# Second half of the recurrence's r and the mLSTM's q and k: blocks of 256 features, with the high and the low input side by side in one product of 512 columns

## The chip, the core and the metric

The kernel runs on one core of a Trainium2 chip. The metric is the device time of one execution in microseconds (us). TensorE (PE in the profile) does the matrix products, VectorE (DVE) and ScalarE (ACT) do the elementwise work, GpSimd (POOL) some small steps, and SyncE (SP) issues the loads of the weights.

## What is computed

One decoder layer in float32, for 256 tokens of 2048 features. This case touches its first part, where one big product `proj = h @ w_in` is cut into columns for two token mixers:

```python
h = rms_norm(x, mix_pre_norm)
proj = h @ w_in
mlstm_p, rwkv_p, gate_p = split_cols(proj, (MLSTM_TOTAL, RWKV_TOTAL, GATE_TOTAL))
q, k, v, o, ir, fr = split_cols(mlstm_p, MLSTM_COLS)          # q, k: 512 columns each
rp = rwkv_p + (shift_right(rwkv_p, 1) - rwkv_p) * mu
r, kr, vr, wl, al, gl = split_cols(rp, RWKV_COLS)             # r, kr, vr: 1024 columns each
...
hm = mlstm_chunkwise(q, k, v, ig, logf)
y = rwkv7_scan(r_h, heads(decay), kr, v_h, kk, kk * a_h)
```

Behind it come the merge of the mixers, cross-attention and a large feed-forward part.

## The kernel before

**Precise products from two halves.** Weights and inputs are split into a high and a low part (`wh`, `wl` and `hx`, which holds `hh` and `hl`; 128x1024 values of weights are one *source*, 512 KB). ACT casts `wh` out of the loaded `raw` (L437), DVE subtracts to get `wl` (L463). Three products are then summed in a PSUM bank: high weights with high input, high with low, low with high. In a feature-major block (`fm`) the weights are the stationary operand and the 256 tokens are the moving columns, so each of the three has 256 columns. In the narrow form a block is 512 features: 8 sources of two 128-row slices (k), and 24 products per source. Token-major blocks (`tm`) move the weights instead, 512 columns at a time.

**The wide form** is used later in the program, by the feed-forward blocks (`fx`) and by `w_mw`: `hx` has high and low input next to each other, so one product of 512 columns covers high weights with both, and one of 256 columns adds low weights with high input. A wide block is 256 features: 4 sources of four k slices, and 16 products per source. Its bank holds two partial sums (for each 128 features), so its evacuation is longer: ACT copies one half out of PSUM, DVE adds the other (function `whole`), and then multiplies.

**Order of the work.** The first blocks are: the small gates (`tm`, 296 columns), r (2 narrow blocks), kr (2), vr (2), q and k of the mLSTM (1 narrow block each, `q_evac`), then v and o (`tm`), the gates and the branches. Sources are numbered in this text from the first one of r: r has 0 to 15, kr 16 to 31, vr 32 to 47, q and k 48 to 63. `Feed` runs ahead: when a source is multiplied, the `wl` of the third one after it is queued on DVE.

**Banks.** The accumulators of these blocks come from a pool of four PSUM banks (`acc`). A narrow or a wide block takes two of them, so a block can only begin when the evacuation of the block two places before it has left its banks.

**Side work.** Everything else (evacuations, the preparation of the recurrence in `k_group`, one for each of four groups of 256 features, and `inverses`) is cut into pieces by generators, and the class `Spread` decides while the program is written out where a piece stands: at each `side.half` at most a few pieces, as long as its budgets for DVE and ACT are positive. It writes pieces out at once, however many there are, where one is needed: `work(b)` begins with `side.need(pend[-2])`, which writes out all that is left of the evacuation two blocks back, and `q_evac` itself starts with

```python
yield from side.patience(tasks["k"], 12)
```

which lets up to 12 pieces pass and then writes out what is left of the last `k_group`. In `k_group`, `kk`, `nr`, `k2` and `ep` are parts of the tile `kt`; a maximum over the head sums `ssk` (from PE) is followed by a logarithm and an exponential on ACT, then by products on DVE that fill `KR` and `BK`, and the scaling of `rr`. `inverses` begins with the products `gramA` of `KR` and `BK` on PE.

Each engine works through its own queue in the order that this made.

Of the kernel before, what the change touches and what calls it, by code (L numbers as in the profile page):

```python
# [15 lines left out]
P = 128  # L16
D = 2048
S = 256
# [136 lines left out]
def _layer(ctx, tc, nc, d, dbg):  # L155
# [9 lines left out]
    def U(name, shape=None, dt=F32):  # L165
        return mp.tile(shape or [P, 8, S], dt, tag="U", bufs=7, name=name)
# [98 lines left out]
    def times(out, ps, row):  # L265

        if len(ps.shape) == 3:
            row = bc(row, ps.shape[1])
        dve.tensor_mul(apart(out), halves(ps), apart(row))

    def whole(ps):

        us, lo = T2("us"), T2("ul")
        for i in range(2):
            act.copy(lo[:, i], ps[i][:, 1])
        for i in range(2):
            dve.tensor_add(us[:, i], ps[i][:, 0], lo[:, i])
        return us

    def bc(ap, n):  # L280
        return ap.unsqueeze(1).broadcast_to((ap.shape[0], n, ap.shape[1]))
# [100 lines left out]
    def block(kind, srcs, xs, evac, before=None, cols=512, pool_=None, pre=None, bankwise=False, tail=0,  # L382
              two=False, wide=None):


        blocks.append(dict(kind=kind, srcs=srcs, xs=xs, evac=evac, before=before, cols=cols,
                           pool=pool_ or acc, pre=pre, task=None, bankwise=bankwise, tail=tail, two=two, wide=wide is not None, xw=wide))
        return blocks[-1]
# [218 lines left out]
    def W(name, blk):  # L607
        return [d[name][blk, c] for c in range(d[name].shape[1])]
# [241 lines left out]

    def r_evac(hf):
        def gen(ps):
            if hf == 0:
                M["rr"] = U("rr")
            for g in range(2):
                pr = PR()
                times(pr, ps[g], st0.rb)
                yield
                for j in range(2):
                    p = hf * 4 + g * 2 + j  # L860
                    shiftmix(M["rr"][:, p], pr[:, j], p)
                yield
        return gen

    def k_evac(hf):
        def gen(ps):
            if hf == 0:
                M["KR"] = big("KR", [P, 8, 4, 2, 64])
                M["BK"] = big("BK", [P, 8, 4, 2, 64])
            kr = M["BK"].rearrange("p a c s t -> p a (c s t)")  # L870
            for g in range(2):
                pr = PR()
                times(pr, ps[g], st0.rb)
                yield
                for j in range(2):
# [304 lines left out]
            tasks["hb"] = side.add(hb_split(), back=True)  # L1180


    def q_evac(i):
        def gen(ps):
            if i == 0:
                yield from side.patience(tasks["k"], 12)
                M["qk"] = U("qk")
            qk = M["qk"]
            for g in range(2):
                o = qk[:, i * 4 + g * 2:i * 4 + g * 2 + 2]  # L1190
                times(o, ps[g], st0.rb)
                yield
            if i == 1:
                side.need(tasks["gates"])
                for _ in range(3):
                    yield
                for h in range(4):
                    q = aux("sc", [P, 384])
                    for jt in range(2):
                        mm(q[:, jt * 256:jt * 256 + 256 - jt * 128], qk[:, 4 + h, jt * 128:(jt + 1) * 128],  # L1200
                           qk[:, h, jt * 128:256])
                    dve.scalar_tensor_tensor(M["pw"][:, h], q, 128 ** -0.5, M["pw"][:, h], op0=ALU.mult, op1=ALU.mult)
                    yield
        return gen
# [294 lines left out]


    block("tm", [d["op"][c, :, :, S:] for c in range(8)], xs0, sm_evac, cols=NSM, pre=pre_sm)
    for hf in range(2):
        block("fm", W("w_in", hf), xs0, r_evac(hf), pre=pre_r0 if hf == 0 else None)
    for hf in range(2):
        block("fm", W("w_in", 2 + hf), xs0, k_evac(hf))
    for hf in range(2):
        block("fm", W("w_in", 4 + hf), xs0, v_evac(hf))

    def drain_bulk():
        while side.bulk:  # L1510
            side._piece(side.bulk[0])

    block("fm", W("w_in", 6), xs0, q_evac(0))
    block("fm", W("w_in", 7), xs0, q_evac(1), )
    for n in range(2):
        block("tm", W("w_in", 8 + n), xs0, vm_evac(n))
    for n in range(2):
        o1 = block("tm", W("w_in", 10 + n), xs0, o_evac(n))

    def need_hb():  # L1520
        for hf in range(2):
# [31 lines left out]
    for i in range(2):  # L1553
        for cb in range(4 + AHEAD):
            if cb >= AHEAD:
                before = None
                if cb == AHEAD:
                    before = need_hb if i else lambda: side.need(o1["task"])
                br = gated(i, cb - AHEAD, before)
            if cb < 4:  # L1560
                block("tm", W("w_in", 12 + i * 4 + cb), xs0, gate_evac(i, cb))
    br["before"] = start_mem

    def load_x():
# [365 lines left out]
def _pairs(w):  # L1930

    return w.reshape(w.shape[0], -1, 256, 2).transpose(0, 1, 3, 2).reshape(w.shape)
# [17 lines left out]
def prepare(i):  # L1950
    f = {k: np.asarray(v) for k, v in i.items()}
    w = f["w_in"][0]
    o = {}
    feat = lambda v: np.ascontiguousarray(v.reshape(S, KD, P).transpose(2, 1, 0))
    o["x"], o["mem"] = feat(f["x"]), feat(f["mem"])
    o["x"] = np.ascontiguousarray(o["x"].reshape(P, 8, 2, S).transpose(1, 0, 2, 3))
    par = np.zeros((P, NPAR), np.float32)

    def put(n, v, rows=P):
        par[:rows, PC[n]:PC[n] + v.shape[1]] = v  # L1960

# [24 lines left out]
    smw = smw.reshape(D, NSM // 2, 2).transpose(0, 2, 1).reshape(D, NSM)  # L1986
    smw = smw.reshape(8, 2, P, NSM).transpose(0, 2, 1, 3)
    o["op"] = np.concatenate([o.pop("x"), smw], 3)
    o["w_s0"] = np.concatenate([par[:, PC["mixg"]:PC["mixg"] + 16], smw[0, :, 0]], 1)
    ga, gb = w[:, 6440:8488], w[:, 8488:10536]  # L1990
    o["w_in"] = _blocks(np.concatenate([w[:, 3080:6152], w[:, 0:1024], _pairs(np.concatenate([w[:, 1024:3072], ga, gb], 1))], 1), 512)
    o["w_up"] = f["rwkv_w_up"][0]
    o["a_up"] = f["rwkv_a_up"][0]
    o["g_up"] = f["rwkv_g_up"][0]
    o["w_br"] = np.concatenate([_blocks(_pairs(f[n][0]), 512) for n in ("w_branch_a", "w_branch_b")], 0)
    o["w_mo"], o["w_mw"] = _blocks(f["w_mix_out"][0][:, :512], 512), _blocks(f["w_mix_out"][0][:, 512:], 256)
    kv = f["xattn_wkv"][0]
    o["w_xk"], o["w_xv"] = _blocks(kv[:, :512], 512), _blocks(_pairs(kv[:, 512:]), 512)
    o["w_xq"] = _blocks(f["xattn_wq"][0], 512)
    o["w_xo"] = _blocks(f["xattn_wo"][0], 512)  # L2000
    fu = f["ffn_w_up"][0].reshape(D, 2, DFF)
    cut = lambda a, b, n: fu[:, :, a:b].reshape(D, 2, -1, n).transpose(0, 2, 1, 3).reshape(D, -1)
    o["w_fu"], o["w_fw"] = _blocks(cut(0, 768, 256), 512), _blocks(cut(768, DFF, P), 256)
    o["w_fd"] = _blocks(_pairs(f["ffn_w_down"][0]), 1024)
    return o
# [15 lines left out]
```

## Time and profile before

| | |
|---|---|
| time, median of 3 runs | 1804.07 us (1803.82 to 1804.76) |
| span of the profiled execution, first to last instruction | 1802.7 us |
| PE busy | 1793.1 us (99%), 11814 products |
| DVE busy | 1325.1 us (74%) |
| ACT busy | 1056.8 us (59%) |
| mean granted TensorE clock | 0.999 |

The page gives the span of the profiled execution and no other time of it; the runs lie 1.1 to 2.1 us above that span. In the page, a row of the table of groups gives the line, the engine, the operation, what it writes and reads, how often, its busy time and the mean of one. Consecutive products overlap in PE, so the duration of one (277 ns) is longer than the distance from its start to the next start; what a product costs is read from the starts. `L68` is the helper through which DVE and ACT instructions are recorded, `L191` that of the products.

### The profile page before, as it was taken

To read this page: it belongs to the slowest core of one execution; us is meant where nothing else is said; L and a number is where in the kernel's file an instruction comes from. 1 tells how busy PE (TensorE), PEld (TensorE's weight loads), DVE (VectorE), ACT (ScalarE), POOL (GpSimd) and SP (SyncE) were. 2 spreads that over 40 slices of the span, in tenths; PEclk is the share of its full clock that TensorE was granted. 3 is DMA by queue.
4 is the path that set the end of the run, shared out by engine and by line. 5 is a ranking of instruction groups with operands and counts; after the bars stand their busy time and mean duration, and the time that the engine had idled before them with its cause. 6 is when DMAs were issued, how large, how long until landed. Compare 5 with 4: busy or idle time off the path is not lost.

```text
span 1802.7 us, 30168 instructions
## 1 busy us (share of the span) xinstructions
PE 1793.1 (99%) x11814; PEld 1636.5 (91%) x11814; DVE 1325.1 (74%) x1948; ACT 1056.8 (59%) x1642; POOL 28.7 (2%) x51
## 2 busy tenths in 40 slices
PE   9999999999999999999999999999999999999998
PEld 8999988888888999899999999999999988888887
DVE  7869995765765768789877788777777775666665
ACT  7576454654554665676666666665565564455454
POOL 0100000100100000000000000000000000000000
PEclk9999999999999999999999999999999999999999
DMA  8656564354556775556666666666666666666664
GB/s 282 206 170 187 164 188 151 120 177 154 188 190 207 246 233 176 187 170 189 210 199 201 208 195 204 209 194 201 207 195 200 205 203 218 208 204 207 201 200 151
DMA packets 99135, 351.61 MB, mean 195 GB/s; under 512 B 10896, under 2 KB 13968, under 8 KB 98864
## 3 DMA queue, kind: packets, MB, share of 16 engines
q1 hardware_dynamic: 97888, 347.38, 60.4%
q8 instruction: 93, 1.52, 0.3%
q0 software_dynamic: 384, 1.18, 0.3%
q10 hardware_dynamic: 720, 1.12, 0.2%
q14 instruction: 50, 0.41, 0.1%
HBM read 347.01 MB, written 2.10 MB: 194 GB/s over the span
## 4 chain that ended last, share of the span: by engine, by line
PE 99%; DVE 0%; DMA 0%; ACT 0%; issue 0%; SPq 0%; DVEq 0%; ACTq 0%
PE fm L191 55%; PE tm L191 39%; PE gram L191 0%; PE Y L191 0%; PE lv L191 0%; DMA op<-in_op_dram 0%; PE X L191 0%; PE num L191 0%; PE zwa L191 0%; PE U L191 0%; PE gramA L191 0%; PE xo L191 0%; PE zg L191 0%; PE Tn L191 0%; PE mT L1353 0%; PE st L191 0%
## 5 line engine op out<-in xcount | busy, mean ns | idle before, releaser
L463 DVE TENSOR_TENSOR wl<-raw,wh 128x1024 fp32r<-128x1024 f32 (+1 forms) x641 | 767.9, 1219 | 145.8 <-ACT wh L437 143.4
L437 ACT CAST wh<-raw 128x1024 fp32r<-128x1024 f32 (+1 forms) x641 | 656.0, 1044 | 109.7 <-PE tm L191 60.7
L191 PE MATMUL fm<-fx,wh 128*128 128x512 f32 (+1 forms) x2240 | 672.8, 364 | 0.6 <-DVE fx L68 0.4
L191 PE MATMUL fm<-fx,wl 128*128 128x256 f32 x2048 | 558.3, 273 | 0.0
L191 PEld LDWEIGHTS fm<-fx,wh 128*128 128x128 f32 x2240 | 409.2, 190 | 49.8 <-DVE fx L68 1.0
L191 PEld LDWEIGHTS fm<-fx,wl 128*128 128x128 f32 x2048 | 393.2, 192 | 0.0
L191 PE MATMUL tm<-wh,as 128*128 128x512 f32 x1024 | 304.6, 379 | 0.0
L191 PE MATMUL tm<-wh,hx 128*128 128x512 f32 (+1 forms) x832 | 243.9, 378 | 1.8 <-ACT hx L68 1.5
L191 PEld LDWEIGHTS tm<-wh,as 128*128 128x128 f32 x1024 | 193.5, 189 | 27.4
L191 PE MATMUL tm<-wl,as 128*128 128x512 f32 x512 | 194.0, 379 | 0.0
L68 ACT COPY ul<-fm 128x256 f32<-128x256 f32 x128 | 44.9, 373 | 225.1 <-PE fm L191 225.1
L191 PE MATMUL fm<-hx,wh 128*128 128x256 f32 x1024 | 174.5, 277 | 0.0
L191 PEld LDWEIGHTS tm<-wh,hx 128*128 128x128 f32 x832 | 151.0, 189 | 22.5 <-POOL wh L450 1.7
L191 PEld LDWEIGHTS fm<-hx,wh 128*128 128x128 f32 x1024 | 155.4, 192 | 1.1
L191 PE MATMUL tm<-wl,hx 128*128 128x512 f32 (+1 forms) x416 | 152.5, 373 | 0.1
L68 DVE TENSOR_TENSOR us<-fm,ul 128x256 f32<-128x256 f32 x128 | 48.5, 421 | 130.9 <-ACT ul L68 130.9
L191 PE MATMUL fm<-hx,wl 128*128 128x256 f32 x512 | 140.8, 275 | 0.0
L68 ACT CAST as<-ac 128x256 fp32r<-128x256 f32 x128 | 45.6, 405 | 153.0 <-PE tm L191 153.0
L68 DVE TENSOR_TENSOR as<-ac,as 128x256 fp32r<-128x256 f32 x128 | 48.6, 422 | 91.3 <-ACT as L68 91.3
L191 PEld LDWEIGHTS tm<-wl,as 128*128 128x128 f32 x512 | 96.8, 189 | 13.7
L191 PEld LDWEIGHTS fm<-hx,wl 128*128 128x128 f32 x512 | 98.3, 192 | 0.0
L191 PEld LDWEIGHTS tm<-wl,hx 128*128 128x128 f32 x416 | 77.5, 189 | 10.7 <-DVE wl L463 0.3
(374 smaller groups left out, 1883.8 us busy)
## 6 DMA issues: line engine op xcount, KB each, us to landing
raw<-in_w_fw_dram SPq DMA_DIRECT2D x232, 512.0 KB, 4.2
raw<-in_w_in_dram SPq DMA_DIRECT2D x160, 512.0 KB, 3.7
raw<-in_w_fd_dram SPq DMA_DIRECT2D x128, 512.0 KB, 4.0
raw<-in_w_br_dram SPq DMA_DIRECT2D x32, 512.0 KB, 4.3
raw<-in_w_mw_dram SPq DMA_DIRECT2D x24, 512.0 KB, 4.6
raw<-in_w_fu_dram SPq DMA_DIRECT2D x24, 512.0 KB, 4.0
raw<-in_w_mo_dram SPq DMA_DIRECT2D x8, 512.0 KB, 4.2
raw<-in_w_xk_dram SPq DMA_DIRECT2D x8, 512.0 KB, 4.3
```

The lines of the kernel that those rows point to most:

```text
L68: return f(out, *a, **k)
L191: pe.matmul(out, lhsT, rhs, start=start, stop=stop, skip_group_check=True)
L437: nc.scalar.copy(o, v)
L463: nc.vector.tensor_sub(o, v, h)
```

## The change

The second half of r (512 features) and q and k of the mLSTM (1024 features) go from three narrow blocks to six wide ones, with their weights in an array of their own (`w_rq`) in blocks of 256 columns. The first half of r, kr and vr stay narrow. The evacuation follows the wide form: a new function, `whole_times`, copies on ACT, adds on DVE and multiplies by the row of inverse norms. The sources keep their numbers and sizes; one of q and k now belongs to one of four blocks (sources 48 to 51, 52 to 55, 56 to 59, 60 to 63).

```diff
+    def whole_times(out, lo, ps, row):
+
+        for i in range(2):
+            act.copy(apart(lo[:, i]), halves(ps[i][:, 1]))
+        for i in range(2):
+            dve.tensor_add(apart(out[:, i]), halves(ps[i][:, 0]), apart(lo[:, i]))
+        dve.tensor_mul(out, out, bc(row, 2))
...
+    def rw_evac(b):
+        def gen(ps):
+            pr = C("pr", "bg1", [P, 2, 2, S])
+            whole_times(pr[:, 0], pr[:, 1], ps, st0.rb)
+            yield
+            for j in range(2):
+                p = b * 2 + j
+                shiftmix(M["rr"][:, p], pr[:, 0, j], p)
+            yield
...
-    def q_evac(i):
+    def q_evac(b):
         def gen(ps):
-            if i == 0:
+            if b == 0:
                 yield from side.patience(tasks["k"], 12)
                 M["qk"] = U("qk")
             qk = M["qk"]
-            for g in range(2):
-                o = qk[:, i * 4 + g * 2:i * 4 + g * 2 + 2]
-                times(o, ps[g], st0.rb)
-                yield
-            if i == 1:
+            whole_times(qk[:, b * 2:b * 2 + 2], T2("ul"), ps, st0.rb)
+            yield
+            if b == 3:
                 side.need(tasks["gates"])
...
+    hxw = lambda k: hx[:, :, k]
+    block("fm", W("w_in", 0), xs0, r_evac(0), pre=pre_r0)
+    for b in range(2):
+        block("fm", W("w_rq", b), xs0, rw_evac(b + 2), cols=256, wide=hxw)
...
-    block("fm", W("w_in", 6), xs0, q_evac(0))
-    block("fm", W("w_in", 7), xs0, q_evac(1), )
+    for b in range(4):
+        block("fm", W("w_rq", 2 + b), xs0, q_evac(b), cols=256, wide=hxw)
```

What this does to the queues is seen at the place where source 56 begins: the second block of q and k before, the third one now. On PE, before (`fm_2190` and `fm_2191` are the banks of the block that ends, `fm_2482` and `fm_2483` those of the one that begins; in brackets the engines whose counters a row waits for):

```order
L191 MATMUL fm_2191<-hx_88,wl_2333 128x256
L191 MATMUL fm_2482<-hx_88,wh_2374 128x256 [waits PE_49,Activation_49]
L191 MATMUL fm_2482<-hx_88,wh_2374 128x256
L191 MATMUL fm_2482<-hx_88,wl_2376 128x256 [waits DVE_49]
L191 MATMUL fm_2482<-hx_88,wh_2374 128x256 x2
L191 MATMUL fm_2482<-hx_88,wl_2376 128x256
L191 MATMUL fm_2483<-hx_88,wh_2374 128x256 [waits PE_49]
```

The first product waits for its weights from ACT, the third for the low weights from DVE; the second bank waits for nothing on DVE. On PE now (`fm_2399` and `fm_2400` are the banks of the block that begins; `ssk` are the head sums of the last `k_group`, `gramA` the first products of `inverses`):

```order
L191 MATMUL ssk_2367<-hsh_2192,bones_77 128x256
L191 MATMUL ssk_2367<-hsl_2193,bones_77 128x256
L191 MATMUL fm_2399<-hx_88,wh_2285 128x512 [waits DVE_49,PE_49]
L191 MATMUL fm_2399<-hx_88,wl_2287 128x256
L191 MATMUL fm_2400<-hx_88,wh_2285 128x512 [waits DVE_49,PE_49]
L191 MATMUL fm_2400<-hx_88,wl_2287 128x256
L191 MATMUL fm_2399<-hx_88,wh_2285 128x512
L191 MATMUL fm_2399<-hx_88,wl_2287 128x256
L191 MATMUL fm_2400<-hx_88,wh_2285 128x512
L191 MATMUL fm_2400<-hx_88,wl_2287 128x256
L191 MATMUL gramA_2425<-BK_1170,KR_1169 64x64 [waits PE_49,Pool_49]
```

The head sums have moved ahead of the block, the `gramA` products into its first source, and the first product into each of the two banks now waits for DVE as well. On DVE, before, from the low weights of source 61 (`wl_2563`) to the evacuation of the first block of q and k (`qk`):

```order
L463 TENSOR_TENSOR wl_2563<-raw_2418,wh_2561 128x1024
L68 TENSOR_TENSOR kt_2170<-kt_2170,at_1458 128x512
L68 TENSOR_TENSOR BK_1251<-kt_2170 64x8x64 x4
L463 TENSOR_TENSOR wl_2599<-raw_2454,wh_2597 128x1024
L68 SCALAR_TENSOR_TENSOR rr_651<-rr_651,par_69,kt_2170 128x256 x2
L68 TENSOR_SCALAR comp_2632<-gramA_2633,con_70 128x8x32
L68 SCALAR_TENSOR_TENSOR comp_2632<-gramA_2633,con_70,comp_2632 128x8x32
L463 TENSOR_TENSOR wl_2654<-raw_2488,wh_2652 128x1024
L68 TENSOR_TENSOR qk_2670<-fm_2190,st0_b_515 128x512
L68 TENSOR_TENSOR qk_2670<-fm_2191,st0_b_515 128x512
```

The last `k_group` is spread out between the low weights, and the evacuation stands behind those of source 63. On DVE now, from the low weights of source 58 (`wl_2347`) to the evacuation of the first of the four blocks:

```order
L471 TENSOR_TENSOR wl_2347<-raw_2222,wh_2345 128x1024
L68 TENSOR_SCALAR kt_2186<-ssk_2367 128x512
L68 TENSOR_TENSOR kt_2186<-kt_2186 128x512
L68 TENSOR_TENSOR KR_1169<-rr_651,kt_2186 128x8x64
L68 SCALAR_TENSOR_TENSOR KR_1169<-kt_2186 128x8x63
L68 TENSOR_TENSOR kt_2186<-BK_1170,kt_2186 128x512
L68 TENSOR_TENSOR kt_2186<-kt_2186,at_1405 128x512
L68 TENSOR_TENSOR BK_1170<-kt_2186 64x8x64 x4
L68 SCALAR_TENSOR_TENSOR rr_651<-rr_651,par_69,kt_2186 128x256 x2
L68 TENSOR_TENSOR qk_2392<-fm_2129,ul_2393 128x256
L68 TENSOR_TENSOR qk_2392<-fm_2130,ul_2393 128x256
```

The whole last `k_group` stands in one piece with no low weights in between, directly ahead of the two adds that empty the banks `fm_2129` and `fm_2130`; the low weights of source 59 come after it.

More of the change, by code (lines that the diff above doesn't have):

```diff
@@ L852, in gen @@
         def gen(ps):
-            if hf == 0:
-                M["rr"] = U("rr")
+            M["rr"] = U("rr")
             for g in range(2):
@@ L859, in gen @@
                 for j in range(2):
-                    p = hf * 4 + g * 2 + j
+                    p = g * 2 + j
                     shiftmix(M["rr"][:, p], pr[:, j], p)
                 yield
+        return gen
+    def rw_evac(b):
[7 more added lines that the diff above has]
+            yield
         return gen
@@ L1501, in _layer @@
     block("tm", [d["op"][c, :, :, S:] for c in range(8)], xs0, sm_evac, cols=NSM, pre=pre_sm)
+    hxw = lambda k: hx[:, :, k]
+    block("fm", W("w_in", 0), xs0, r_evac(0), pre=pre_r0)
+    for b in range(2):
+        block("fm", W("w_rq", b), xs0, rw_evac(b + 2), cols=256, wide=hxw)
     for hf in range(2):
-        block("fm", W("w_in", hf), xs0, r_evac(hf), pre=pre_r0 if hf == 0 else None)
+        block("fm", W("w_in", 1 + hf), xs0, k_evac(hf))
     for hf in range(2):
-        block("fm", W("w_in", 2 + hf), xs0, k_evac(hf))
-    for hf in range(2):
-        block("fm", W("w_in", 4 + hf), xs0, v_evac(hf))
+        block("fm", W("w_in", 3 + hf), xs0, v_evac(hf))
     def drain_bulk():
@@ L1511, in drain_bulk @@
             side._piece(side.bulk[0])
-    block("fm", W("w_in", 6), xs0, q_evac(0))
-    block("fm", W("w_in", 7), xs0, q_evac(1), )
+    for b in range(4):
+        block("fm", W("w_rq", 2 + b), xs0, q_evac(b), cols=256, wide=hxw)
     for n in range(2):
-        block("tm", W("w_in", 8 + n), xs0, vm_evac(n))
+        block("tm", W("w_in", 5 + n), xs0, vm_evac(n))
     for n in range(2):
-        o1 = block("tm", W("w_in", 10 + n), xs0, o_evac(n))
+        o1 = block("tm", W("w_in", 7 + n), xs0, o_evac(n))
     def need_hb():
@@ L1560, in _layer @@
             if cb < 4:
-                block("tm", W("w_in", 12 + i * 4 + cb), xs0, gate_evac(i, cb))
+                block("tm", W("w_in", 9 + i * 4 + cb), xs0, gate_evac(i, cb))
     br["before"] = start_mem
@@ L1990, in prepare @@
     ga, gb = w[:, 6440:8488], w[:, 8488:10536]
-    o["w_in"] = _blocks(np.concatenate([w[:, 3080:6152], w[:, 0:1024], _pairs(np.concatenate([w[:, 1024:3072], ga, gb], 1))], 1), 512)
+    o["w_rq"] = _blocks(np.concatenate([w[:, 3592:4104], w[:, 0:1024]], 1), 256)
+    o["w_in"] = _blocks(np.concatenate([w[:, 3080:3592], w[:, 4104:6152], _pairs(np.concatenate([w[:, 1024:3072], ga, gb], 1))], 1), 512)
     o["w_up"] = f["rwkv_w_up"][0]
```

## The prediction

> **What bounds the kernel now.** I read the page first (busy shares, clock, chain), then who waits for whom on PE, then the order of both kernels where the new blocks begin, and last the timelines of DVE, ACT and PE at that place.
>
> ```profile
> PE 1793.1 (99%) x11814; PEld 1636.5 (91%) x11814; DVE 1325.1 (74%) x1948; ACT 1056.8 (59%) x1642; POOL 28.7 (2%) x51
> PEclk9999999999999999999999999999999999999999
> PE tm L191 <- ACT hx L68: 1.5, 1, 1.5
> PE sum L191 <- ACT turn L68: 0.9, 1, 0.9
> PE warm L191 <- POOL mhalf L215: 0.9, 1, 0.9
> PE fm L191 <- DVE fx L68: 0.4, 1, 0.4
> PE X L191 <- DVE so L68: 0.3, 1, 0.3
> PE xo L191 <- ACT xv L68: 0.2, 1, 0.2
> ```
>
> PE is the bound from end to end at full clock, and all its waits come to 4.2 us. So the time is what PE's queue takes, plus every wait that is added to it; nothing behind can give such a wait back, since PE is full to the end. DVE has 26% left over the whole span, but not here: the columns of the next table are PE, PEld, DVE, ACT and POOL, busy us with the count behind.
>
> ```profile
> 165.00:175.00 10.00, 10.00 (x92) 10.00 (x91) 8.80 (x12) 8.15 (x13) 0.00 (x0) 1.00 0.71 227
> 175.00:190.00 15.00, 15.00 (x136) 15.00 (x136) 13.99 (x19) 9.58 (x15) 1.17 (x2) 1.00 0.56 180
> 190.00:205.00 15.00, 15.00 (x198) 14.36 (x196) 14.78 (x22) 6.96 (x8) 2.21 (x4) 1.00 0.56 164
> ```
>
> While PE multiplies q and k, DVE is idle for 1.2, 1.0 and 0.2 us in these stretches. It keeps up, with little to spare.
>
> **The products.** PE's starts give the price. The first pair of rows is the first and the last of 28 rows of this form in the r blocks, the second pair the first and the last of 29 in a wide block.
>
> ```profile
> 39.93 0.39 PE L191 MATMUL fm<-hx,wh 128*128 128x256 f32 x2
> ...
> 48.97 0.39 PE L191 MATMUL fm<-hx,wh 128*128 128x256 f32 x2
> 899.67 0.38 PE L191 MATMUL fm<-fx,wh 128*128 128x512 f32 x1
> ...
> 908.84 0.38 PE L191 MATMUL fm<-fx,wh 128*128 128x512 f32 x1
> ```
>
> Narrow: (48.97 - 39.93) / 27 = 0.3348 us for three products of 256 columns. Wide: (908.84 - 899.67) / 28 = 0.3275 us for 512 and 256. A gain of 0.0073 us. There are 16 k slices x 4 tiles of 128 features x 3 replaced blocks = 192 of them: 1.4 us less. The columns streamed are the same; only one start in three goes. [...]
>
> **The evacuations.** Rows of the same operations elsewhere:
>
> ```profile
> L68 ACT COPY ul<-fm x128: 372/373/379, 637.7 to 1463.5; 128x256 f32<-128x256 f32 x128
> L68 DVE TENSOR_TENSOR us<-fm,ul x128: 414/422/428, 638.1 to 1463.9; 128x256 f32<-128x256 f32 x128
> L68 DVE TENSOR_TENSOR us<-us,stf_b x58: 691/693/694, 867.0 to 1464.4; 128x512 f32<-128x512 f32 x58
> L68 DVE TENSOR_TENSOR qk<-fm,st_b x4: 677/683/689, 200.9 to 213.3; 128x512 f32<-128x512 f32 x4
> ```
>
> For 256 features DVE had one multiplication, 0.68 us; now it has two adds and one, 2 x 0.42 + 0.69 = 1.54, so 0.85 more; ACT has two copies, 0.75 more. Six blocks: 5.1 us more on DVE and 4.5 on ACT. ACT has the room (24.7 of 40 us busy in the table above, with its casts ahead of need). For r I cost it at nothing: PE's own work hides it, and the order has no new wait of PE there. The loads are the same 512 KB sources in the same number, and SP's and POOL's queues keep their rows: nothing.
>
> **The wait.** Four banks hold two wide blocks. The third block of q and k needs the banks of the first at once, 10.5 us after that block ended (2 x 16 x 0.3275), where the narrow form gave 21. The order shows the price: at source 56 PE's first product now waits for DVE's add out of `fm_2129`, and that add stands behind the whole last `k_group`, written out in one piece. When does PE arrive? Before, at 183.23, one source ahead of the head sums:
>
> ```profile
> 183.23 0.39 PE L191 MATMUL fm<-hx,wh 128*128 128x256 f32 x2
> ...
> 185.91 0.29 PE L191 MATMUL ssk<-hsh,bones 128*128 128x256 f32 x1
> 186.03 0.28 PE L191 MATMUL ssk<-hsl,bones 128*128 128x256 f32 x1
> ...
> 186.39 0.28 PE L191 MATMUL fm<-hx,wh 128*128 128x256 f32 x1
> ```
>
> By then 128 of the 192 triples have given 0.9 us, and the head sums (186.39 - 185.91 = 0.48) now come first: arrival at 182.8. When does DVE arrive? These are its rows of before for the same work, with the one ACT row that it waits for:
>
> ```profile
> 175.39 0.69 DVE L68 TENSOR_SCALAR kt<-ssk 128x512 f32<-128x512 f32 x1 [0.81 <-PE ssk L191]
> 187.47 0.68 DVE L68 TENSOR_SCALAR kt<-ssk 128x512 f32<-128x512 f32 x1
> 188.07 1.22 DVE L463 TENSOR_TENSOR wl<-raw,wh 128x1024 fp32r<-128x1024 f32 x1
> 188.19 1.30 ACT L68 ACTIVATE kt<-kt 128x512 f32<-128x512 f32 x2 [3.83 <-DVE kt L68]
> 189.52 0.69 DVE L68 TENSOR_TENSOR kt<-kt 128x512 f32<-128x512 f32 x1 [0.23 <-ACT kt L68]
> 191.93 1.21 DVE L463 TENSOR_TENSOR wl<-raw,wh 128x1024 fp32r<-128x1024 f32 x1
> 193.07 0.68 DVE L68 TENSOR_TENSOR kt<-kt,at 128x512 f32<-128x512 f32 x1
> 193.85 2.60 DVE L68 TENSOR_TENSOR BK<-kt 64x512 f32<-64x512 f32 x4
> 196.48 1.23 DVE L463 TENSOR_TENSOR wl<-raw,wh 128x1024 fp32r<-128x1024 f32 x1
> 197.62 0.88 DVE L68 SCALAR_TENSOR_TENSOR rr<-rr,par,kt 128x256 f32<-128x256 f32 x2
> 198.41 0.68 DVE L68 TENSOR_SCALAR comp<-gramA,con 128x256 f32<-128x256 f32 x1
> ```
>
> From one maximum (175.39) to the next (187.47) the new order has the same rows less one subtraction of low weights, so the second maximum starts at 186.3 (187.47 - 1.14) if the first starts when it did. The two ACT functions behind the first maximum now stand ahead of the cast of source 56, which can cost their 1.3 us: 187.6. I take the middle, 187.0. From there without the low weights: maximum 0.68, ACT and back 189.52 - 188.15 = 1.37 (nothing fills it now), four products 191.93 - 189.52 = 2.41, one product 0.78, `BK` 2.63, `rr` 0.79, one add 0.42: 9.1 us. DVE frees the bank at 196.1. PE, there at 182.8, waits **13.3 us**. Queued behind that product on PE are the rest of the block, `gramA` and all blocks after, and they wait with it; DVE and ACT wait for `gramA` in turn, but have other rows ahead of it. What was late before, the low weights, is not late next: after the wait PE has three sources (3 x 8 x 0.3275 = 7.9 us) before it needs those of source 59, and DVE has the second add, the second block's evacuation and that subtraction, some 3.3 us.
>
> **The clock after the wait.** The trace shows PE cold twice, at the start and after the last product (the seventh number of the last row is the granted clock):
>
> ```profile
> 0.89 3.35 PE L191 MATMUL warm<-ones 128*128 128x128 f32 x14 [0.89 <-POOL mhalf L215]
> 788.04 1.72 PE L191 MATMUL warm<-ones 128*128 128x128 f32 x14
> 4.34 1.04 PE L191 MATMUL tm<-wh,hx 128*128 128x296 f32 x4
> 5.60 0.29 PE L191 MATMUL tm<-wh,hx 128*128 128x296 f32 x1
> 1796.76 1.12 PE L191 MATMUL sum<-z,turn 128*128 128x512 f32 x2 [0.92 <-ACT turn L68]
> 1800.00:1803.00 3.00, 0.00 (x0) 0.00 (x0) 0.00 (x0) 0.00 (x0) 0.00 (x0) 0.50 0.26 94
> ```
>
> The same 14 products take 3.35 us at the start and 1.72 later: half speed. It lasts from 0.89 into the group at 4.34, about 3.6 us. At the end the clock is down to 0.50 within 3 us of the last product. So 13.3 us of waiting end at half clock, and about 3.6 us of half speed lose 1.8 us. Bounds: nothing, if the clock stays, and 3.6 us, if it needs twice that time.
>
> [...]
>
> **The sum.** Profiled span 1802.7; - 1.4 + 13.3 + 1.8 = 1816.4. The median of the runs lies 1.37 us above the span, so on its scale 1804.1 + 13.7 = **1817.8 us**, slower by 0.8%. 0.2%, 3.6 us, is about what a measurement of this kernel can tell from no change.
>
> **The other ways.**
> - *A shorter wait.* DVE makes use of all its idle time from 165 to 190 (2.2 us) and the clock stays: 1804.1 - 1.4 + 11.1 = 1813.8. For it: 0.81 of that idle time is a wait for head sums that now come earlier. Against: the order forces the chain with ACT.
> - *A longer half clock.* It lasts twice the 3.6 us of the start and loses 3.6 instead of 1.8: 1819.6. For it: the trace has just one warm-up, which may have been a lucky one. Against: that one is all there is to go by. [...]
> - *A second wait.* DVE has 4 x 0.85 = 3.4 us more for q and k in a stretch where it was 92 to 99% busy; if PE catches up with it and all of this lands on PE, 1821.2. For it: the table of windows. Against: low weights have some microseconds of cover right after the wait.
> - *Not slower.* The bank is free when PE comes, since DVE gets to the adds 13 us sooner than I count; only the 1.4 us remain, 1802.7, within 0.2%. It decides where wait and clock together come to 5.0 us (5.0 - 1.4 = 3.6). For it: PE waited nowhere here before, and DVE is idle a quarter of the whole span. Against: from 165 to 190 DVE has only 2.2 us of idle time from which to come sooner.
> - *That the wide product brings nothing*: 1.4 us, inside the range of all the above.
>
> **Chances.** The forecast 0.60; shorter wait 0.12; longer half clock 0.12; second wait 0.11; not slower 0.05. The range holds the first four with the bounds of the unknown parts (start of the maximum 186.3 to 187.6, clock 0 to 3.6): from 1812 to 1822.5, and leaves out the last and the tails of the others. Faster by more than 0.2% would take 3.6 us where 1.4 are to be had: 0.01. Same 0.05, slower 0.94.
>
> **What the changed profile will show.** Right: in the list of waits one new entry, PE `fm` behind DVE `qk`, once, 12 to 15 us, near 183; PE's busy share down by about that; DVE without low weights between maximum and adds; a granted clock of about one half for a few microseconds after; triples of 0.3275 us in the r and q blocks; and from 230 on the same work as before, shifted. Wrong: no such entry, or one under 5 us; then DVE came to the last `k_group` earlier than I count. A series of short waits for low weights behind source 59 would show the second wait.

## The result, and the profile after

| | before | after |
|---|---|---|
| time, median (the kernel before was measured again beside) | 1803.95 us (1803.82 to 1804.76) | 1819.87 us (1819.09 to 1820.55) |
| ratio | 1 | 1.0086, 95% interval 1.0074 to 1.0098 |
| span of the profiled execution | 1802.7 us | 1817.9 us |
| mean granted clock | 0.999 | 0.995 |

The change made the kernel 15.9 us slower (0.9%); 1817.8 was predicted, with a range of 1812.0 to 1822.5. Two parts of the page after, and three rows of the list of PE's waits (us in total, times, longest):

```profile
PE 1793.9 (99%) x11622; PEld 1631.5 (90%) x11622; DVE 1329.3 (73%) x1960; ACT 1059.0 (58%) x1654; POOL 28.6 (2%) x51
PEclk9999899999999999999999999999999999999999
...
PE fm L191 <- DVE qk L68: 15.4, 1, 15.4
PE tm L191 <- ACT hx L68: 1.1, 2, 0.8
PE tm L191 <- DVE wl L471: 0.2, 1, 0.2
```

One long entry is new and it is nearly the whole loss: PE waits once, 15.4 us, for DVE's `qk`. It lies just outside the 12 to 15 us that the prediction named as the sign of being right. The 192 products fewer are there (11622 against 11814). The same three stretches as before, columns PE, PEld, DVE, ACT, POOL, then the granted clock:

```profile
165.00:175.00 10.00, 10.00 (x67) 9.31 (x66) 9.30 (x14) 8.81 (x15) 0.00 (x0) 1.00 0.68 189
175.00:190.00 15.00, 7.49 (x48) 6.73 (x46) 12.04 (x17) 7.07 (x11) 1.16 (x2) 0.85 0.50 157
190.00:205.00 15.00, 7.12 (x78) 6.04 (x80) 11.76 (x20) 6.03 (x12) 2.21 (x4) 0.58 0.21 68
```

PE stands still for half of the last two stretches. DVE, on whose work PE waits, is not full either: 12.0 and 11.8 of 15 us, against 14.0 and 14.8 before. It works through a chain, alone and with ACT. The timelines of PE, then DVE, then ACT there:

```profile
182.21 0.28 PE L191 MATMUL ssk<-hsl,bones 128*128 128x256 f32 x1
197.88 0.77 PE L191 MATMUL fm<-hx,wh 128*128 128x512 f32 x1 [15.39 <-DVE qk L68]
198.65 0.63 PE L191 MATMUL fm<-hx,wh 128*128 128x512 f32 x1
...
199.29 0.63 PE L191 MATMUL fm<-hx,wh 128*128 128x512 f32 x1
...
175.88 0.68 DVE L68 TENSOR_SCALAR kt<-ssk 128x512 f32<-128x512 f32 x1
178.85 1.23 DVE L471 TENSOR_TENSOR wl<-raw,wh 128x1024 fp32r<-128x1024 f32 x1 [2.29 <-ACT wh L445]
...
188.68 0.69 DVE L68 TENSOR_SCALAR kt<-ssk 128x512 f32<-128x512 f32 x1
190.72 0.69 DVE L68 TENSOR_TENSOR kt<-kt 128x512 f32<-128x512 f32 x1 [1.36 <-ACT kt L68]
...
196.52 0.88 DVE L68 SCALAR_TENSOR_TENSOR rr<-rr,par,kt 128x256 f32<-128x256 f32 x2
197.32 0.75 DVE L68 TENSOR_TENSOR qk<-fm,ul 128x256 f32<-128x256 f32 x2
...
176.60 1.29 ACT L68 ACTIVATE kt<-kt 128x512 f32<-128x512 f32 x2 [1.36 <-DVE kt L68]
177.79 1.03 ACT L445 CAST wh<-raw 128x1024 fp32r<-128x1024 f32 x1
```

PE's last head sums start at 182.21, and the next product only at 197.88, behind DVE's first add out of the bank (197.32). DVE gets to the last `k_group` (the maximum at 188.68) late, because at 178.85 it had waited 2.29 us for the cast of source 56, which ACT takes up only after the two functions of the group before (176.60). After the wait the pairs of products stand 0.64 us apart (199.29 - 198.65) instead of 0.3275: half clock. How long, the granted clock shows:

```profile
185.37:202.43 17.06, 4.55 (x40) 3.87 (x40) 14.36 (x25) 5.72 (x11) 2.21 (x4) 0.50 0.20 61
202.43:206.00 3.57, 3.57 (x51) 3.06 (x48) 2.04 (x4) 1.04 (x1) 0.00 (x0) 0.99 0.42 142
```

PE works 4.55 us of it at half speed, from 197.88 to 202.43, and so loses 2.3 us. The products themselves are as cheap as forecast; these are the first and the last of 33 rows of this form in r's two wide blocks, (53.68 - 43.20) / 32 = 0.3275:

```profile
43.20 0.38 PE L191 MATMUL fm<-hx,wh 128*128 128x512 f32 x1
...
53.68 0.38 PE L191 MATMUL fm<-hx,wh 128*128 128x512 f32 x1
```

All waits of PE come to 19.1 us against 4.2: 14.9 more. With 2.3 for the clock and 1.4 less for the products that is 15.8, between the difference of the spans (15.2) and that of the medians (15.9).

One forecast of the changed profile held only later than it said: "from 230 on the same work as before, shifted". PE's transposes `haT` start 21.0 us later than before (352.5 against 331.5), the transposes `mT` 15.3 us later (549.1 against 533.8). Until about 350 us PE does its side products in another order.

### The profile page after: what moved, and what is told of

Read it like the earlier page. It is cut to its first block, busy times and chain, and to the rows that moved or that the text cites. A ratio compares the mean times of both kernels' runs of the same rounds, so it can differ in the third digit from the quotient of the medians.

```text
span 1817.9 us, 29798 instructions
## 1 busy us (share of the span) xinstructions
PE 1793.9 (99%) x11622; PEld 1631.5 (90%) x11622; DVE 1329.3 (73%) x1960; ACT 1059.0 (58%) x1654; POOL 28.6 (2%) x51
## 4 chain that ended last, share of the span: by engine, by line
PE 98%; DVE 1%; DMA 0%; ACT 0%; issue 0%; DVEq 0%; ACTq 0%
PE fm L191 55%; PE tm L191 38%; PE gram L191 0%; PE Y L191 0%; DMA op<-in_op_dram 0%; PE lv L191 0%; PE num L191 0%; DVE BK L68 0%; PE X L191 0%; PE gramA L191 0%; PE zwa L191 0%; PE U L191 0%; PE xo L191 0%; PE zg L191 0%; PE Tn L191 0%
## 5 line engine op out<-in xcount | busy, mean ns | idle before, releaser
L191 PE MATMUL fm<-hx,wh 128*128 128x256 f32 (+1 forms) x832 | 174.2, 303 | 15.4 <-DVE qk L68 15.4
L191 PEld LDWEIGHTS fm<-hx,wh 128*128 128x128 f32 x832 | 134.0, 192 | 21.8 <-issue 15.6
L191 PEld LDWEIGHTS tm<-wl,as 128*128 128x128 f32 x512 | 96.8, 189 | 13.7
```

The costliest lines, as they stand in the source:

```text
L191: pe.matmul(out, lhsT, rhs, start=start, stop=stop, skip_group_check=True)
```

## Experiments

The theory, A: the loss is one bank, which DVE frees only behind the last `k_group`, written out in one piece because the block two places later needs the bank. Its rival B: the wide form's longer evacuation overloads DVE. Theory C: the half clock behind the wait is a loss of its own. Times below are set against the kernel before in the same comparison, whose median lay between 1803.95 and 1804.55 us.

### e1 and e2: one part alone

e1 keeps q and k as before, and only the second half of r is wide; e2 the reverse. The lines that choose the blocks (the evacuations and the cut of the weights follow them):

```diff
...
-    for b in range(4):
-        block("fm", W("w_rq", 2 + b), xs0, q_evac(b), cols=256, wide=hxw)
+    for i in range(2):
+        block("fm", W("w_in", 5 + i), xs0, q_evac(i))
...
```
```diff
...
-    block("fm", W("w_in", 0), xs0, r_evac(0), pre=pre_r0)
-    for b in range(2):
-        block("fm", W("w_rq", b), xs0, rw_evac(b + 2), cols=256, wide=hxw)
+    for hf in range(2):
+        block("fm", W("w_in", hf), xs0, r_evac(hf), pre=pre_r0 if hf == 0 else None)
...
```

> Only the second half of r is wide; q and k are the two narrow blocks of the kernel before. Theory A (the loss is the bank of the first q and k block, which DVE frees only behind the whole last k_group): nothing of it is left; no wait of PE at source 56, PE waits 4 us in all, and 64 triples gain 0.5 us: 1803.5 us. Rival B (the wide form itself costs, by its longer evacuation on DVE and ACT): two of the six blocks cost a third of the loss, so about 1809 us, with short waits of PE for low weights behind r.

> Only q and k are wide, in four blocks; r is narrow as before. Theory A: the whole loss stands: one wait of PE for DVE qk at source 56 of 15 us, the clock at half for 4 to 5 us behind it, and 128 triples gain 0.9 us instead of 1.4: 1820.3 us. Rival B: four of the six blocks' longer evacuations cost two thirds of the loss: about 1814.5 us.

e1: 1805.06 us against 1804.50, ratio 1.0004 (0.9995 to 1.0013), no difference. e2: 1816.25 us, ratio 1.0064 (1.0049 to 1.0080). So the loss needs q and k in the new blocks, as A says, but a quarter of it goes with r. The waits of e1 and then of e2, with DVE's two maxima and the stretch of half clock in e2:

```profile
PE tm L191 <- DVE wl L471: 0.8, 2, 0.6
...
PE fm L191 <- DVE qk L68: 11.2, 1, 11.2
172.34 0.69 DVE L68 TENSOR_SCALAR kt<-ssk 128x512 f32<-128x512 f32 x1
...
185.19 0.69 DVE L68 TENSOR_SCALAR kt<-ssk 128x512 f32<-128x512 f32 x1
185.49:199.14 13.65, 4.75 (x41) 3.95 (x41) 10.79 (x19) 5.72 (x11) 2.21 (x4) 0.50 0.24 68
```

In e2 both maxima stand 3.5 us earlier than in the changed kernel (172.34 and 185.19 against 175.88 and 188.68). From one to the other is as long, 12.85 against 12.80 us. With r wide the later side work stands one place behind: in the order of e2 the third group's maximum follows the low weights of source 54, in the changed kernel those of source 55. Alone this costs e1 a wait for low weights of 0.8 us; ahead of a bank that is needed at once it costs 3.6 us (1819.87 against 1816.25; 4.2 by the distances to the kernel before). Why the order shifts was not tested; r's longer evacuation, which is charged to the same budgets as the side work, is the likely reason.

### e3: four blocks, without the demand for the bank

```diff
-                    if kj + 1 < s.shape[1] and (not b["wide"] or kj % 2):
+                    if kj + 1 < s.shape[1] and (b["cols"] != 256 or kj % 2):
...
-            whole_times(qk[:, b * 2:b * 2 + 2], T2("ul"), ps, st0.rb)
+            times(qk[:, b * 2:b * 2 + 2], ps[0], st0.rb)
...
-        block("fm", W("w_rq", 2 + b), xs0, q_evac(b), cols=256, wide=hxw)
+        block("fm", W("w_rq", 2 + b), xs0, q_evac(b), cols=256)
```

The first line leaves the places where side work may stand as they are in the wide blocks.

> As the changed kernel, but the four q and k blocks of 256 features use three products of 256 columns each, all in one bank per block, and an evacuation of one multiplication as before. The order of the side work is kept: the last k_group is still written out in one piece two blocks later. What goes is the demand for the first block's bank, since four blocks now have four banks. Theory A: no wait at the first product of source 56; PE goes on until it needs something that is queued behind the forced k_group (gramA for BK, or the low weights of source 59, some 5 to 8 us later), so a wait of 6 to 10 us there or two smaller ones: 1810 to 1816 us. Rival A2 (the demand for the bank is only the first of several and all of the piece is hidden otherwise): no wait over 1 us, 1803.6 us. Rival B (the surplus of DVE work by the wide evacuation is what makes DVE late): also no wait, 1803.6 us, and then the runs e1 and e2 tell A2 from B.

1812.07 us against 1804.50, ratio 1.0042 (1.0028 to 1.0056). PE no longer stops at source 56. It goes on through source 56 and half of 57, and stops at 189.8 us, at `gramA` products in the middle of source 57, which need `BK` out of the forced piece; the clock falls there too:

```profile
PE gramA L191 <- DVE BK L68: 5.6, 2, 4.8
194.62 0.45 PE L191 MATMUL gramA<-BK,KR 64*64 64x64 f32 x2 [4.85 <-DVE BK L68]
194.00:200.83 6.83, 5.45 (x52) 4.95 (x53) 6.77 (x12) 1.67 (x2) 0.00 (x0) 0.51 0.07 7
```

Here q and k have no wide product and no longer evacuation (r's second half still has), yet half of the loss stays, 7.6 us. B cannot explain it, nor can A2, by both of which 1803.6 was due. What costs is the `k_group` in one piece, brought about by a block that comes two places later after 10.5 us. The bank adds the rest by stopping PE earlier. How much of e3's 7.6 us goes with r was not separated.

### e4, e6: the wait filled

Products of ones, read by nothing, stand ahead of source 56 (e4 52 calls, e6 65):

```diff
-        block("fm", W("w_rq", 2 + b), xs0, q_evac(b), cols=256, wide=hxw)
+        block("fm", W("w_rq", 2 + b), xs0, q_evac(b), cols=256, wide=hxw,
+              before=(lambda: keep_warm(65)) if b == 2 else None)
```

> The changed kernel with 52 products of 128 columns of ones (into a bank of their own, read by nothing) ahead of the first product of source 56, where PE waits for the bank. At full clock they take 52 x 1.72/14 = 6.4 us by the group of 14 at 788. Theory C (the half clock behind the wait costs time): PE idles 9 us instead of 15.4; if the clock falls only after some 3 us without products and PE still idles longer than that, half clock is left in part; if the filled time shortens the half clock to nothing, about 1817.6 us, 2.3 us less than the changed kernel. Rival D (the record of half clock is no loss of time, or the fill doesn't reach): 1819.9 us, unchanged. The wait for DVE itself ends at the same time, 197.9 us into the span, by both.

> As e4, but the fill is as long as the wait: 130 products of 128 columns, by the 104 of e4 (11.77 us) 14.7 us, so that PE idles 0.7 us instead of 3.7. Theory C (the clock falls where one whole window of 3.41 us passes without products, and comes back at the end of the first busy one; all half stretches in the records of the changed kernel and of e2, e3 and e4 are 5, 4, 2 and 1 times 3.413 us long): no half clock at all; the changed kernel ran 4.55 us at half after its wait and loses 2.3 us by it, so 1817.6 us. Rival D (the half clock is a record of idleness and costs nothing, or the restart itself is slow whatever came before): 1819.9 us.

e4: 1819.66 us, ratio 1.0085 (1.0071 to 1.0098), e6: 1817.84 us, ratio 1.0076 (1.0061 to 1.0090). e4's text counted the products wrongly: the trace has 104, not 52, and they filled 11.8 us. The waits and stretches of e4, then of e6:

```profile
PE fm L191 <- DVE qk L68: 3.7, 1, 3.7
194.50:197.91 3.41, 0.00 (x0) 0.00 (x0) 3.38 (x7) 1.04 (x2) 0.00 (x0) 0.99 0.00 0
197.91:201.33 3.42, 3.14 (x14) 2.43 (x16) 3.35 (x7) 0.00 (x0) 0.00 (x0) 0.51 0.00 0
...
PE fm L191 <- DVE qk L68: 0.8, 1, 0.8
182.00:206.00 24.00, 23.23 (x257) 21.92 (x256) 21.86 (x36) 8.78 (x15) 2.33 (x5) 1.00 0.27 87
```

In e4 PE was idle for 3.7 us, the clock fell after 3.4 of them, and PE got back to work at half clock (198.19 to 201.33, 3.1 us instead of 4.55). That is 0.7 us less lost, and the time is 0.2 to 0.8 lower; for C it decides little. In e6 the clock stays whole, and the time is 2.0 us under the changed kernel's by the medians, 2.5 by the distances to the kernel before in each comparison (13.4 against 15.9); 2.3 was expected. C is right: the half clock is a loss, of some 2 us, and not just a record of idleness.

### e7: the cast ahead of the side work

```diff
                 feed.lo(i + 1)
+                if b.get("early"):
+                    feed.hi(i + 3)
                 side.half(True)
...
-        block("fm", W("w_rq", 2 + b), xs0, q_evac(b), cols=256, wide=hxw)
+        block("fm", W("w_rq", 2 + b), xs0, q_evac(b), cols=256, wide=hxw)["early"] = True
```

> The changed kernel, but in the four q and k blocks the cast of the source three ahead is queued on ACT before the side work of that half, not behind it. The cast of source 56 then stands ahead of the two functions of the third k_group, which wait for its maximum. Theory A with the order of ACT as the cause of the 2.3 us by which the second maximum was later than predicted (188.7 against 186.4 to 187.0): DVE no longer waits 2.29 us for that cast, the second maximum starts at 186.4, the bank is free at 195.5, PE waits 13.1 us instead of 15.4, and the time is 2.3 us less, 1817.6 us (0.8 either way, by where the restart falls against the steps of the clock). Rival E (DVE is late by the amount of its own work, and the wait for the cast is slack): another wait of DVE takes its place, and the time stays at 1819.9 us.

1818.69 us, ratio 1.0079 (1.0066 to 1.0092).

```profile
PE fm L191 <- DVE qk L68: 13.5, 1, 13.5
176.46 0.68 DVE L68 TENSOR_SCALAR kt<-ssk 128x512 f32<-128x512 f32 x1
177.06 1.22 DVE L471 TENSOR_TENSOR wl<-raw,wh 128x1024 fp32r<-128x1024 f32 x1
...
187.18 0.69 DVE L68 TENSOR_SCALAR kt<-ssk 128x512 f32<-128x512 f32 x1
184.94:202.01 17.07, 5.62 (x43) 4.73 (x44) 14.05 (x25) 5.72 (x11) 2.21 (x4) 0.50 0.19 64
```

The time is 0.3 us above the upper end of what was expected (1817.6, 0.8 either way). DVE's wait for the cast is gone: the low weights follow the maximum at once, and from one maximum to the next it is 10.7 us (187.18 - 176.46) instead of 12.8. The first maximum comes 0.6 us later than in the changed kernel (176.46 against 175.88), so the second one is 1.5 us earlier, not 2.3. PE's wait is 1.9 us shorter. The clock gives back less: PE starts 1.5 us earlier, but the clock comes back at nearly the same time (202.01), so 5.6 us run at half instead of 4.55 and lose 0.5 us more. Rival E is out, and the 2.3 us come down to 1.2 in the time (1.6 by the distances to the kernel before).

### e5: the bank emptied in a step of its own

```diff
...
+    def q_scale(b, us):
+        if b == 0:
+            yield from side.patience(tasks["k"], 12)
+            M["qk"] = U("qk")
+        dve.tensor_mul(M["qk"][:, b * 2:b * 2 + 2], us, bc(st0.rb, 2))
+        yield
...
-            if b == 0:
-                yield from side.patience(tasks["k"], 12)
-                M["qk"] = U("qk")
+            if b < 2:
+                us = apart_sum(ps)
+                yield
+                tasks["qs", b] = side.add(q_scale(b, us), back=True, ahead_of=tasks["inv"])
+                return
+            yield from side.patience(tasks["qs", 1], 12)
```

`apart_sum` holds the copies and adds of `whole_times`, without the multiplication.

> The changed kernel, but the first two q and k blocks leave their banks in a step of their own (the ACT copies and the DVE adds, into two tiles), which does not wait for the last k_group; a second step, behind that k_group, multiplies into qk. All products are wide as in the changed kernel, DVE and ACT do the same instructions, only in another order, and the last k_group is spread over the low weights of sources 60 to 63 again. Theory A (the whole loss is the bank behind the k_group in one piece): no wait of PE over 1 us between 160 and 230, no half clock, 1802.7 to 1803.5 us, so the same as before or up to 1.4 us faster. Rival B (the longer evacuation of the wide form has DVE late as well): low weights come late one after the other; the surplus of DVE for the four blocks, 3.4 us, lands on PE: about 1806 us.

1805.93 us against 1804.41, ratio 1.0009 (0.9999 to 1.0018). The wait for the bank and the half clock are gone, and with them 14.4 of the 15.9 us, though all blocks are still wide. That settles A for the loss. But the time is the 1806 that B named, and not the 1802.7 to 1803.5 of A: the kernel is not faster than before. PE's first product of v starts at 208.41 against 210.24 before, so the wide form is 1.7 us ahead at that place (191.64 against 193.38 from the first product of r). Then this is lost again: from there to the transposes `haT` near 332 us e5 takes 124.4 us and the kernel before 121.2. The waits of e5, a row of DVE and the stretch from 205 to 255 in e5, and the same row and stretch in e1 and in the kernel before:

```profile
PE tm L191 <- DVE wl L471: 1.7, 4, 0.6
216.96 1.24 DVE L68 STREAM_TRANSPOSE A<-comp 128x1024 f32<-128x1024 f32 x1
205.00:255.00 50.00, 49.60 (x261) 42.30 (x260) 48.21 (x92) 17.42 (x19) 0.00 (x0) 1.00 0.59 178
...
213.62 1.23 DVE L68 STREAM_TRANSPOSE A<-comp 128x1024 f32<-128x1024 f32 x1
205.00:255.00 50.00, 50.00 (x278) 44.30 (x278) 48.23 (x92) 16.86 (x17) 0.00 (x0) 1.00 0.60 182
...
208.43 1.25 DVE L68 STREAM_TRANSPOSE A<-comp 128x1024 f32<-128x1024 f32 x1
205.00:255.00 50.00, 50.00 (x281) 44.46 (x281) 46.38 (x91) 18.02 (x19) 0.00 (x0) 1.00 0.57 178
```

DVE has 48.2 of 50 us to do, 1.8 more than before, and its low weights come late three times between 253 and 262. That is B's picture, 50 us behind the place where B was looked for. But the longer evacuation of q and k is not what fills this stretch: e1, whose q and k are narrow, has the same 48.2 us there. What e1 and e5 share is side work that stands later. In `inverses` a transposition on DVE follows the `gramA` products, and a long chain of small products follows that; it starts at 208.43 before, at 213.62 in e1 and at 216.96 in e5.

### e8, e9, e10: where the gain of the wide form goes

e8 is e5 with the multiplications on POOL, e9 is e5 with the casts of e7 in the blocks of q, k, v and o, e10 has both:

```diff
-        dve.tensor_mul(out, out, bc(row, 2))
+        pool.tensor_mul(out, out, bc(row, 2))
...
```

> As e5, but the six wide evacuations of r, q and k multiply by the row of inverse norms on POOL instead of DVE; DVE keeps the adds only, 0.84 us per block against 0.68 of the narrow form. POOL is busy 28.6 us of the whole span and has nothing else here but small steps. In e5 PE was 1.7 us ahead of the kernel before when q and k ended, and then lost 3.2 us on late low weights in the token-major blocks up to 262, while DVE was 95 to 98% busy (before: 88 to 97%). Theory F (these late low weights are the wide evacuations' surplus on DVE, 5.1 us in all): six multiplications of 0.69 us, 4.1 us, leave DVE, the waits for low weights go back to nothing, and 1.4 to 1.7 us of the wide products are left as a gain: 1802.7 to 1803.2 us, against 1804.4 before. Rival G (the late low weights come from the changed order of the side work, not from its amount): the same waits as in e5, 1805.9 us. Rival H (POOL's multiplications slow DVE down or hold qk back): waits for qk or longer DVE rows beside POOL's, over 1806 us.

> e5 (banks emptied in a step of their own, all on DVE) with the casts of e7 (queued ahead of the side work) in the blocks of q, k, v and o. In e5 DVE waited 2.29 us for a cast at 191 and 1.67 us for one at 259, both behind side work on ACT. Theory F (DVE has too much to do from 205 to 255): it gets 2.3 us earlier, which the 3.2 us of late low weights are then less by, if nothing else holds it in between: 1803.5 to 1804.5 us. Rival I (between 205 and 255 DVE waits for the head sums and the products of PE anyway, so an earlier start is lost there): only the last of the three waits shrinks, 1805.3 us.

> e8 (multiplications of the wide evacuations on POOL) with the casts of e9. In e8 one wait of PE for low weights, 1.3 us at 199.6, came from the 2.3 us wait of DVE for a cast at 191 and from two DVE rows that took 1.76 and 2.30 us beside POOL's multiplications instead of 0.68 and 1.22; another, 0.7 us at 260.8, from a wait of DVE for a cast. Theory F: both go or halve, and nearly all of the 1.4 us of the wide products is left: 1802.8 to 1804 us, the fastest of all. Rival H (POOL beside DVE is what costs): the wait at 199.6 stays, 1805 to 1806 us.

e8: 1805.67 us against 1804.55, ratio 1.0005 (0.9996 to 1.0014). e9: 1804.98 against 1804.33, 1.0002 (0.9993 to 1.0011). e10: 1804.40 against 1804.33, 1.0000 (0.9991 to 1.0009). None can be told from the kernel before, and none reached the time by which its run would have borne out F (1802.7 to 1803.2, 1803.5 to 1804.5, 1802.8 to 1804). How far PE was ahead of the kernel before (minus) or behind it, in us, each counted from its own first product of r:

| | e1 | e5 | e8 | e9 | e10 |
|---|---|---|---|---|---|
| first product of v | -0.69 | -1.74 | -0.34 | -1.77 | -1.65 |
| first transpose `haT`, near 332 us | +0.36 | +1.42 | +0.89 | +0.48 | +0.16 |

At the last product of the program each stands within 0.1 us of its second row, so all is decided between 208 and 332 us. All five lose their lead there, e1 too. Waits and DVE and POOL rows of e8, then a wait and an ACT row of e10, then that ACT row in the kernel before:

```profile
PE fm L191 <- DVE wl L471: 1.2, 1, 1.2
PE tm L191 <- DVE wl L471: 0.8, 2, 0.6
196.87 1.76 DVE L68 TENSOR_TENSOR kt<-kt,at 128x512 f32<-128x512 f32 x1
198.56 2.30 DVE L471 TENSOR_TENSOR wl<-raw,wh 128x1024 fp32r<-128x1024 f32 x1
208.42 1.20 DVE L471 TENSOR_TENSOR wl<-raw,wh 128x1024 fp32r<-128x1024 f32 x1
...
196.37 3.40 POOL L1213 TENSOR_TENSOR qk<-qs,st_b 128x512 f32<-128x512 f32 x2
208.57 2.20 POOL L286 TENSOR_TENSOR qk<-qk,st_b 128x512 f32<-128x512 f32 x1 [7.70 <-DVE qk L68]
...
PE gram L191 <- ACT bg L68: 0.3, 1, 0.3
256.13 1.11 ACT L68 COPY Lt<-L 128x512 f32<-128x512 f32 x1 [7.63 <-DVE tmp L68]
...
252.69 1.11 ACT L68 COPY Lt<-L 128x512 f32<-128x512 f32 x1 [7.72 <-DVE tmp L68]
```

In e8 the late low weights of v and o shrink (from 1.7 to 0.8 us in the list). That does not bear F out: PE itself comes to v 1.4 us later than in e5, which gives DVE that time, and without its multiplications DVE is as busy from 205 to 255 as with them (48.2 us in e8, 48.1 in e10). H has a share: beside POOL's two multiplications, two rows of DVE take 1.76 and 2.30 us instead of 0.68 and 1.22, and a new wait of 1.2 us for low weights follows them. It needs DVE's 2.3 us wait for a cast as well: e5 has that wait (at 193.3) without the long rows, e10 such long rows (2.30 us at 196.29) without the wait, and neither has PE waiting there. The casts of e9 and e10 leave a wait of `gram` for an ACT copy. In e10 it is 0.3 us in the list and 1.0 by the starts (3.33 us from the last product before `gram` to the first behind it, 2.29 before). The casts did not cause it: the copy stands in ACT's order where it stood before, but the copies `Lt` ahead of it wait for DVE's chain in `inverses`, which ends some 3.4 us later (256.13 against 252.69).

So the rows speak for rival G, the changed order of the side work, more than for F, its amount. What moves the order, r's wide half or the budgets of `Spread`, was not tested, and no version without any such wait was tried. All that one could win, 1.4 to 1.7 us, is about what a measurement can tell (0.1%, 1.8 us).

## Why the prediction was right, and where it was off

- *The products*: -1.4 forecast. The pair of products takes 0.3275 us as in the feed-forward blocks, and e5 shows PE 1.7 us ahead at the end of q and k. Right, though no kernel here kept it to the end.
- *Arrival of PE* at 182.8: its last head sums start at 182.21, and the next product could have started at 182.3. Right within 0.5 us.
- *The chain of DVE* from the second maximum to the first add done: 9.1 forecast; 197.32 + 0.42 - 188.68 = 9.06. Right.
- *The second maximum* at 187.0, bounds 186.3 to 187.6: it came at 188.68, outside the bounds. This is the term that was mis-sized. Of the 1.7 us, 0.5 is the first maximum, which was taken from the kernel before (175.39) and came at 175.88; the other 1.2 lie between the two. The prediction saw that two functions of ACT now stand ahead of the cast of source 56, and let that cost their 1.3 us, or half of it. But ACT cannot begin them before DVE's maximum is done, and DVE then waits for both and for the cast behind them: 2.29 us in the trace. The subtraction for source 56 stands in DVE's queue between maximum and next product, and its input in ACT's queue behind the two functions that lie between them. e7 takes the wait away, and the two maxima stand 10.7 us apart; the prediction's lower bound had 10.9. So the wait of PE was 15.4 instead of 13.3, with PE 0.5 us early and DVE 1.7 us late. Of the 2.1 us by which the sum was short (15.8 against 13.7), this is nearly all: the clock took 0.5 more than forecast, and the other waits shrank by 0.5. The time stayed in the range all the same, because the range also left room for a longer half clock and a second wait.
- *The half clock*: 1.8 forecast, bounds 0 to 3.6. By the clock it was 2.3, and e6 without it is 2.0 to 2.5 us faster. The right size, and not the whole 3.6 of the rival. That the half clock lasts twice the 3.6 us of the start, on which the upper bound and that rival rest, was the author's estimate, and no run shows it: the work at half clock came to 4.55 us in the changed kernel and to 5.6 us at most (e7).
- *No second wait*: right, the low weights of source 59 cost 0 and one later wait 0.2 us. Low weights do come late where there is no such wait, in e5, but from 253 us on, and by the order of the side work more than by DVE's 3.4 us of added work.
- *r costed at nothing*: wrong as a reason, though it didn't move the sum, which took the places in the order from the changed kernel as a whole. With r wide the later side work stands one source later, and 3.6 of the 15.9 us go with it (e1, e2).
- The rivals: the shorter wait's 11.1 us were 4.3 too few; the longer half clock's time (1819.6) is the measured one, but by another way: longer wait, not longer cold clock. "Not slower" would have needed DVE 15 us earlier than it came.

## What to carry to other kernels

Smaller blocks with as many banks each need their banks back sooner: compare the time until the bank is needed again with the longest piece of work that the scheduler puts ahead of its evacuation, and separate the emptying of a bank from whatever else the evacuation waits for (14.4 of 15.9 us came back so). When a queue's order puts the two halves of a chain through two engines around another engine's input, count the whole round trip as its delay, and not the added instructions. A saving on the bound engine can come back as waits where an engine that feeds it is nearly full (DVE before: 88.4 of the 95 us from 165 to 260) and the change moves side work to a later place: five kernels here lost a lead of 0.3 to 1.8 us in this way. Compare PE's place at two or three landmarks, not only the list of waits, to see where.

## What the runs showed of the hardware

- In these runs the distances between changes of the clock were multiples of 3.413 us. The five stretches of half clock were 17.06 (changed kernel), 13.65 (e2), 6.83 (e3), 3.42 (e4) and 17.07 us (e7) long, which are 5, 4, 2, 1 and 5 times 3.413 within 0.01 us. In the changed kernel the clock's record in the trace has 180.91 us from the start of full clock to its fall, 17.07 from there to its return and 1614.50 to its fall at the end, which are 53, 5 and 473 such steps. The length of the wait alone did not set how much half clock it left: 15.4 us of waiting left 4.55 us of work at half in the changed kernel, 13.5 us left 5.6 in e7, and 3.7 us left 3.1 in e4.
- The 3.41 us ahead of a fall of the clock were empty of products in e4 (194.50 to 197.91), as the text of e6 has it, but not in every run: in the changed kernel those up to 185.37 held products until 182.5, 0.5 us of work, and in e7 those up to 184.94 held 1.4; the clock fell in both. At half clock, 3.41 us with 2.2 us of work (195.18 to 198.59 in e7) did not bring the full clock back, and 3.42 us with 3.1 (197.91 to 201.33 in e4) did.
- Beside multiplications on POOL some rows of DVE took longer, and some did not. In e8 the two multiplications of 128x512 on POOL at 196.37 took 1.70 us each, and two rows of DVE beside them 1.08 us longer each (1.76 and 2.30 us instead of 0.68 and 1.22). One multiplication, at 208.57, took 2.20 us where DVE's subtraction had begun first (208.42) and took its usual 1.20. The two rows of DVE with an input from PSUM that follow beside it (`comp`, from 209.55 on) took 0.66 and 0.73 us, against 0.67 and 0.73 before. Why one row was held up and another not, the runs do not show.
